# A hybrid attention and linear-attention layer on one core: the first prompt outputs placed later, gate logits in a projection bank, mean squares in PSUM, zero matmuls at the head, later conversions

## The chip, the core and the metric

The kernel runs on one core of a Trainium2 chip. The core has five engines with instruction queues of their own: TensorE (PE in the profile; its weight loads are shown as PEld), VectorE (DVE), ScalarE (ACT), GpSimd (POOL) and SyncE (SP), which issues most of the DMAs. Operands lie in SBUF, matmuls write to PSUM, which here has eight banks of 128 partitions by 512 fp32 numbers. The metric is the time of one execution on the device in microseconds, lower is better; the median of the runs counts.

## What is computed

One step of a one-layer encoder over a prompt of 2048 tokens and a sample of 32, width 1024, all in fp32. Cut to what matters:

```python
def prompt_layer(x, p):
    qa, ka, va, qg, kg, vg, rg, log_a = mixer_inputs(rmsnorm(x, g_mix), w_in, w_alpha, b_alpha, g_q, g_k)
    ...
    attn_o = sink_attend(q_blk, k_band, v_band, sinks, mask)      # 8 query heads, 2 KV heads, window 128, chunks of 64
    gla_o, s_final = gla_chunked(qg, kg, vg, log_a, s0)           # 4 heads, keys 64, values 128, state 64 x 128
    h = x + concat(attn_o, rmsnorm(gla_o, g_gla_out) * silu(rg)) @ w_out
    return h + square(relu(rmsnorm(h, g_ffn) @ w_up)) @ w_down    # 1024 -> 4096 -> 1024
```

`mixer_inputs` is one product with `w_in` (1024 x 2320) whose columns are the attention's q, k and v (512, 128, 128), the linear attention's q, k, v and output gate (256, 256, 512, 512) and 16 columns from which `w_alpha` makes the forget gate: `log_a = log_sigmoid(ca @ w_alpha + b_alpha) / 16`. Queries and keys of the attention get an RMS norm per head. The sample runs the same layer with a cache of 128 keys and a given state.

## The kernel before

Numbers are split in two parts (h and l) and each product takes three matmuls (hh, lh, hl), so that a projection of one tile of 128 tokens over 1024 inputs is 24 matmuls. Tokens go in 16 prompt tiles (0 to 15) and the sample's tile (16).

The program runs through these stages, each recorded with generators that hand control back (`yield`):

- **Attention phase**, to about 368 us. Per tile: `zq` (queries, 24 matmuls of 512 columns), `zkv` (keys, values and the gate's 16 columns, 272 columns of a bank of 512), `zr` (output gate of the linear attention). `self.rsqrt` (L257 to L262) makes the norms of queries and keys by three rounds of small DVE operations on ten numbers a token; its mean squares `ss` lie in an SBUF tile (tag `ssqk`), its scratch in columns 272 to 281 of the zkv bank. `attend(t)` then makes the transposes `qTp` and `kTp`, the scores `S_0` and `S_1` of the two chunks, softmax (`mx`, `negm`, `P`, `es`), the transposes `pT` and the outputs `O`.
- **Linear attention (GLA) phase**, to about 660 us. Eight halves h of two prompt tiles each (h = 0 has the sample's tile in front). Per half: `zq_0`, `zq_1`, `zk_0`, `zk_1`, evacuated by DVE into `kq` (L947), `zv` per tile, evacuated by ACT into `v`; `la`, the gate's logits from `decay(h)`: one bank, evacuated by ACT into `cc`, then log-sigmoid on ACT and a cumulative sum on DVE (L874, L878). Per tile `gla_tile`: decay factors `E` (POOL differences, ACT exponentials, DVE products at L1033 and L1037), the score blocks `A` (104 small matmuls), masked copies into `AT`, output `go` with the state update, and an RMS norm of `go` that writes `g` (L1146) and so empties the banks of `go`; `gTp` transposes `g`.
- **Op phase**, to about 860 us: product with `w_out`, residual, and the second RMS norm, whose square sums are added over partitions by a ones-matmul (`oprb`) and turned by transposes (`rsq_y`).
- **FFN phase**, to 2148 us: up and down products in a Strassen-like scheme of blocks over three groups of tokens; `load_tok` fetches the next group's blocks `T` and ACT and POOL split them into h and l.

What sets the order: `_pe` chains every matmul to the one recorded before it, so TensorE runs in the order of recording. A generator that yields n continues when the matmuls recorded since have a cost of n by the kernel's own counter (`self.clock`, in ns, added to by each matmul recorded). DVE, ACT, POOL and SP take their order from the scheduler. In the first two phases projections take PSUM banks from a pool of three (`ps_m`), everything else from a pool of five (`ps_s`); a tile waits until the last reader of the tile that had the bank is done. Weights and inputs come by DMA through SP's queue; POOL also adds up weight blocks for the FFN (`sd`) and issues its own DMAs.

Of the kernel before, what the change touches and what calls it, by code (L numbers as in the profile page):

```python
# [66 lines left out]
class Builder:  # L67
# [241 lines left out]
    def attention_phase(self):  # L309
# [3 lines left out]
        with ExitStack() as ctx:  # L313
# [56 lines left out]
            V.memset(self.ones, 1.0)  # L370
# [511 lines left out]
    def gla_phase(self):  # L882
        tc, a, V, S, G, Q = self.tc, self.a, self.V, self.S, self.G, self.Q
        nt = self.nt
        with ExitStack() as ctx:
# [375 lines left out]
    def op_phase(self, pool):  # L1261
# [155 lines left out]
        for j, (p, gi) in enumerate(groups):  # L1417
# [37 lines left out]
    def ffn_phase(self):  # L1455
# [4 lines left out]
        with ExitStack() as ctx:  # L1460
# [220 lines left out]
            def load_tok(e, x, engs):  # L1681
# [3 lines left out]
                for i, eng in enumerate(engs):  # L1685
                    ks = slice(i * H // len(engs), (i + 1) * H // len(engs))
                    S.activation(h[:, ks], f32(l[:, ks]), AF.Copy)
                    eng.tensor_tensor(out=l[:, ks], in0=f32(l[:, ks]), in1=f32(h[:, ks]), op=ALU.subtract)
# [424 lines left out]
```

## Time and profile before

| | |
|---|---|
| runs | median 2156.96 us, 2151.72 to 2158.32, 3 runs |
| profiled execution | 2154.14 us, its span 2152.1 us, mean granted TensorE clock 0.995 |
| busy | PE 2121.8 us, DVE 1510.1, ACT 1246.6, POOL 1509.1 |
| DMA | 398.60 MB, mean 185 GB/s |
| end of the attention phase, of GLA, start of the FFN | about 368, 660 and 860 us |

How to read the rows that follow: a row of the timeline has the start and the duration in us, the engine, the line, the operation, "out<-in", sizes, and, in brackets, how long the engine stood idle before it and what it waited for. A row of the table by windows has the busy time of PE, PEld, DVE, ACT and POOL with the count of instructions, then the granted TensorE clock (1.00 is full speed), the DMA share and GB/s. A row of the groups has the busy time, the mean in ns, and the idle time before. Matmuls overlap in the pipeline, so the distance between two starts is what one costs, not its duration.

### The profile page before, as it was taken

The page shows a single profiled execution, that of the slowest core. Times are in us where ns is not written, and L with a number is a line of the kernel's source. Part 1 is how long each engine was busy: PE and PEld are TensorE (multiplying, and loading weights), DVE is VectorE, ACT ScalarE, POOL GpSimd, SP SyncE. Part 2 cuts the span into 40 slices and gives each one's busy share as a digit, 9 for nine tenths or more (in the row PEclk, how much of TensorE's full clock was granted, in tenths as well). Part 3 has the DMA queues.
Part 4 walks back from the last instruction along what each step waited for, and adds up shares of the span by engine and source line. Part 5 has one row for each costly group of instructions (what it writes and reads, how often), then busy time and mean ns, then how long its engine had stood idle before and what let it go on. Part 6 is the DMA issues. An engine that isn't in the chain of part 4 may idle for free.

```text
span 2152.1 us, 40745 instructions
## 1 busy us (share of the span) xinstructions
PE 2121.8 (99%) x14826; PEld 1998.8 (93%) x14826; DVE 1510.1 (70%) x3381; ACT 1246.6 (58%) x2773; POOL 1509.1 (70%) x1423
## 2 busy tenths in 40 slices
PE   8999998999999999999999999999999999999999
PEld 7777786788889999999999999999999999999998
DVE  7777776789897444677777766666666657776665
ACT  6555555665564223766666666656655666666663
POOL 2455656645452667888887887788887768888887
PEclk9999999999999999999999999999999999999999
DMA  7465667353447888755554576444444674444443
GB/s 280 171 206 174 223 225 228 113 170 134 165 149 262 322 339 307 254 176 172 162 161 142 159 257 220 127 136 140 139 140 127 205 260 138 142 151 155 141 127 107
DMA packets 195786, 398.60 MB, mean 185 GB/s; under 512 B 32753, under 2 KB 117922, under 8 KB 188802
## 3 DMA queue, kind: packets, MB, share of 16 engines
q1 hardware_dynamic: 160802, 339.88, 47.0%
q10 hardware_dynamic: 28224, 27.77, 3.8%
q0 software_dynamic: 6560, 28.35, 3.5%
q8 instruction: 117, 1.92, 0.4%
q14 instruction: 83, 0.68, 0.1%
HBM read 290.79 MB, written 105.15 MB: 184 GB/s over the span
## 4 chain that ended last, share of the span: by engine, by line
PE 88%; DVE 4%; ACT 3%; DMA 3%; issue 1%; SPq 0%; ACTq 0%; POOL 0%; DVEq 0%; POOLq 0%
PE dn L171 29%; PE u L171 29%; PE op L171 8%; PE zq L171 4%; PE zr L171 4%; PE zv L171 4%; PE zkv L171 2%; PE zk L171 2%; PE go L171 1%; PE O L171 1%; PE S L171 1%; PE A L171 1%; PE pT L175 1%; DMA wop<-in_w_out 1%; DVE AT L1102 0%
## 5 line engine op out<-in xcount | busy, mean ns | idle before, releaser
L1690 DVE TENSOR_TENSOR P<-P,dn 128x712 f32<-128x712 f32 (+1 forms) x613 | 535.1, 874 | 240.3 <-PE dn L171 224.1
L44 ACT ACTIVATE u<-u 128x356 f32<-128x356 f32 (+1 forms) x384 | 174.0, 453 | 35.9 <-PE u L171 22.9
L44 ACT ACTIVATE r<-u 128x356 f32<-128x356 f32 (+1 forms) x189 | 87.2, 461 | 122.9 <-PE u L171 122.7
L1690 DVE TENSOR_TENSOR u<-u,r 128x356 f32<-128x356 f32 (+1 forms) x144 | 75.8, 526 | 116.4 <-PE u L171 98.8
L1583 POOL TENSOR_TENSOR stage<-stage 128x512 f32<-128x512 f32 x90 | 116.5, 1294 | 20.9 <-DMA stage<-in_w_up 14.2
L795 POOL TENSOR_TENSOR sd<-sd 128x128 f32<-128x128 f32 (+2 forms) x132 | 99.3, 759 | 32.9 <-DMA sd<-in_w_down 29.4
L1026 POOL TENSOR_TENSOR E<-cc 128x256 f32<-128x256 f32 (+1 forms) x117 | 69.6, 630 | 73.4 <-DVE cc L878 24.3
L1102 DVE COPY_PREDICATED AT<-masks,A 64x64 f32<-64x64 int32 (+1 forms) x330 | 82.9, 253 | 17.2 <-ACT AT L44 6.9
L1690 DVE TENSOR_TENSOR uT<-u,uT 128x356 fp32r<-128x356 f32 (+1 forms) x183 | 90.1, 511 | 2.9 <-ACT uT L44 2.7
L44 ACT ACTIVATE uT<-u 128x356 fp32r<-128x356 f32 (+1 forms) x187 | 81.7, 458 | 3.3 <-DVE u L1690 2.8
L1690 DVE TENSOR_TENSOR uB<-u,uB 128x356 fp32r<-128x356 f32 (+1 forms) x141 | 72.4, 513 | 14.1 <-ACT u L44 13.9
L44 ACT ACTIVATE op<-y 128x356 f32<-128x356 f32 (+1 forms) x42 | 19.6, 468 | 96.5 <-DVE y L1430 96.4
L1430 DVE TENSOR_TENSOR y<-op,y 128x356 f32<-128x356 f32 (+1 forms) x48 | 25.2, 532 | 68.2 <-PE op L171 63.6
L44 ACT ACTIVATE P<-S,negm 128x192 f32<-128x192 f32 (+2 forms) x128 | 51.5, 417 | 36.3 <-DVE negm L656 30.3
L44 ACT ACTIVATE E<-E 128x1024 f32<-128x1024 f32 (+2 forms) x68 | 67.2, 1012 | 1.1
L44 ACT ACTIVATE uB<-u 128x356 fp32r<-128x356 f32 (+1 forms) x141 | 64.5, 458 | 2.9
L1037 DVE TENSOR_TENSOR E<-E,kq 128x256 f32<-128x256 f32 (+1 forms) x117 | 57.3, 542 | 0.6 <-ACT E L44 0.5
L44 ACT ACTIVATE v<-go 128x256 f32<-128x256 f32 (+1 forms) x34 | 12.8, 380 | 66.2 <-DVE Sp L1134 32.7
L620 POOL COPY VB<-v 64x64 f32<-64x64 f32 x64 | 15.0, 234 | 49.2 <-ACT v L44 47.1
L44 ACT ACTIVATE pS<-pT 128x256 f32<-128x256 f32 (+1 forms) x62 | 27.5, 488 | 32.0 <-PE pT L175 31.9
L655 DVE TENSOR_REDUCE mx<-S 128x2 f32<-128x384 f32 (+2 forms) x64 | 32.8, 536 | 18.5 <-PE S L171 18.1
L1690 DVE TENSOR_TENSOR u<-u,f 128x356 f32<-128x356 f32 (+1 forms) x86 | 44.7, 519 | 1.4 <-ACT u L44 1.4
(1577 smaller groups left out, 8158.4 us busy)
## 6 DMA issues: line engine op xcount, KB each, us to landing
stage<-in_w_up SPq DMA_DIRECT2D x90, 512.0 KB, 4.3
stage<-sd SPq DMA_DIRECT2D x86, 512.0 KB, 4.5
stage<-in_w_down SPq DMA_DIRECT2D x43, 512.0 KB, 3.3
stage<-su SPq DMA_DIRECT2D x30, 512.0 KB, 4.1
stage<-in_w_down SPq DMA_DIRECT2D x47, 256.0 KB, 3.4
sd<-sd POOLq DMA_DIRECT2D x11, 1024.0 KB, 5.3
x1a<-in_x_prompt SPq DMA_DIRECT2D x16, 512.0 KB, 6.2
wod<-wop SPq DMA_DIRECT2D x16, 512.0 KB, 3.1
```

The lines of the kernel that those rows point to most:

```text
L44: ins = f(*args, **kw)
L171: self._pe(self.T.matmul(out, lhsT, rhs, start=start, stop=stop, **kw), ns)
L175: self._pe(self.T.transpose(out=out, in_=in_, identity=self.ident[:r, :r]), 109)
L620: G.tensor_copy(vb[hp, ch, cs], v[ch * 64 : ch * 64 + 64, cs])
L655: V.reduce_max(mx[:, ch, us], sp, axis=AX.X)
L795: self.after(self.G.tensor_tensor(out=o, in0=x, in1=y, op=op), self.last_pe)
L1026: G.tensor_tensor(out=e4, in0=c4, in1=ref, op=ALU.subtract)
L1037: V.tensor_tensor(out=e4, in0=e4, in1=halves_of(kq, L, m), op=ALU.mult)
L1102: V.copy_predicated(dst, mk.unsqueeze(1).broadcast_to([L // nh, 2, w // m, m]), src[r].rearrange("s p (n m) -> s p n m", m=m),)
L1430: self.after(V.tensor_tensor(out=y[:, f], in0=ps, in1=y[:, f], op=ALU.add), self.last_state if j == 0 else None)
L1583: tt = lambda o, x, y, op: G.tensor_tensor(out=o, in0=x, in1=y, op=op)
L1690: add = lambda out, x, y, op=ALU.add: V.tensor_tensor(out=out, in0=x, in1=y, op=op)
```

## The change

Eight edits.

1. *Head.* A tile of zeros is cleared by DVE, and three fp32 matmuls of 128 x 384 on it stand ahead of the first projection; their result is not used. The transposed input of the first two tiles comes in four pieces of two k-slices each instead of two of four.
2. *Mean squares.* `ss` of the query and key norms lies in columns 288 to 297 of the zkv bank, in PSUM.
3. *Attention's last tile.* `attend(15)` yields 11000 instead of 8500.
4. *GLA's first prompt tile.* The step that makes `go_0` yields 13000 instead of 10000.
5. *Gate logits.* For halves of 256 tokens `la` takes a bank of the pool of three (`ps_m`).
6. *Op phase.* In the second of its groups (j = 1) the three steps of the norm of the group before stand behind output blocks 2, 3 and 5.
7. *Conversions.* `load_tok` issues the DMA as before, but the splits of the next group's blocks are recorded four units later.
8. *End.* The two halves of the last unit have banks of their own.

```diff
@@ attention phase, head
+            warm = self.mid.tile([P, 576], F32, tag="cc", name="warm")[:, :512]
+            V.memset(warm, 0.0)
+            idle = self.ps_s("idle")
+            for _ in range(3):
+                self.mm(idle[:, :384], warm[:, :P], warm[:, :384], True, True)
...
-            half = [slice(0, 4), slice(4, KB)]
-            fetch_x = lambda t, i: Q.dma_start(xT[t][:, half[i]], a["xT_prompt"][t, :, half[i]])
+            two = [slice(k, k + 2) for k in range(0, KB, 2)]
+            fetch_x = lambda t, i: Q.dma_start(xT[t][:, two[i]], a["xT_prompt"][t, :, two[i]])
...
+            for i in range(KB // 2):
+                fetch_x(0, i)
+                fetch_q(2 * i)
+                fetch_x(1, i)
+                fetch_q(2 * i + 1)
@@ norms of queries and keys
-                ss = self.small.tile([P, 10], F32, tag="ssqk", name=f"ssqk_{t}")[:r]
+                ss = bank[:r, 288:298]
@@ attend
-                yield 8500 if t else 12500
+                yield {0: 12500, nt - 1: 11000}.get(t, 8500)
@@ decay
-            x = self.ps_s(f"la_{h}")
+            x = self.ps_m(f"la_{h}")
@@ gla_tile
-                yield 10000 if t != nt - 1 else 5000
+                yield 5000 if t == nt - 1 else 13000 if first else 10000
@@ op phase
-                if f in ((1, 2, 4) if gi else (1, 2, 5)) and pending is not None:
+                if f in ((2, 3, 5) if j == 1 else (1, 2, 4) if gi else (1, 2, 5)) and pending is not None:
@@ FFN phase
+            def load_tok(e, x, engs, delay=0):
                 h, l = e.T[x]
                 Q.dma_start(f32(l), self.Td[e.p][x])
...
+                if delay:
+                    fresh.append([delay, convert])
+                else:
+                    convert()
...
-                        load_tok(envs[n + 1], t, (G, G))
+                        load_tok(envs[n + 1], t, (G, G), 4)
...
+                        if end:
+                            ps = [x.tile([P, 512], F32, tag="b", name=f"dn{g}_{q}_{j}").unsqueeze(1) for x in ps1[:2]]
...
                 merge_some(g % NF, i, x)
+                convert_due()
```

Where the moved steps stand now. First TensorE's rows at the end of the attention phase; `S_1` is tile 14's, `qTp` and `kTp` are tile 15's. Before:

```order
L171 MATMUL S_1_0_4375<-kW_4233,qT_4227 128x192
L171 MATMUL S_1_1_4376<-kW_4233,qT_4227 128x192
L175 MATMUL qTp_4397<-packed,qk_4128 128x128 x4
L175 MATMUL kTp_4402<-packed,kn_4259 128x128
L175 MATMUL kTp_4402<-packed,CA_385 96x128
L171 MATMUL zr_4370<-wr0h,nT_14h 128x512
L171 MATMUL zr_4370<-wr0l,nT_14h 128x512
```

and of the change, where the first three zr rows shown are the last of twelve behind S_1:

```order
L171 MATMUL zr_4363<-wr1h,nT_14h 128x512
L171 MATMUL zr_4363<-wr1l,nT_14h 128x512
L171 MATMUL zr_4363<-wr1h,nT_14l 128x512
L175 MATMUL qTp_4405<-packed,qk_4122 128x128 x4
L175 MATMUL kTp_4410<-packed,kn_4252 128x128
L175 MATMUL kTp_4410<-packed,CA_395 96x128
L171 MATMUL zr_4363<-wr1h,nT_14h 128x512
```

Twelve zr matmuls have come between the scores of tile 14 and the transposes of tile 15. Behind them S_0 of tile 15 stands after pT_1 of tile 14, S_1 after zq_1, and la after that, ahead of all 24 zk_0.

Next TensorE's rows at the first prompt tile of GLA (`go_0` is tile 0's output, `A_1` tile 1's score blocks). Before:

```order
L171 MATMUL A_1_5245<-E_0_4955 64x32
L171 MATMUL go_0_5266<-v_4872,AT_4697 128x128
L171 MATMUL go_0_5267<-v_4872,AT_4697 128x128
L171 MATMUL go_0_5266<-v_4872,AT_4697 128x128
L171 MATMUL go_0_5267<-v_4872,AT_4697 128x128
L171 MATMUL go_0_5267<-v_4872,kdT_5029 64x128 x4
L171 MATMUL A_1_5244<-E_0_4955 64x32
```

and of the change:

```order
L171 MATMUL A_1_5238<-E_1_4959 64x32
L171 MATMUL zv_5346<-wvg0h,nTb_1h 128x512
L171 MATMUL zv_5346<-wvg0l,nTb_1h 128x512
L171 MATMUL zv_5346<-wvg0h,nTb_1l 128x512
L171 MATMUL zv_5346<-wvg0h,nTb_1h 128x512
L171 MATMUL zv_5346<-wvg0l,nTb_1h 128x512
L171 MATMUL zv_5346<-wvg0h,nTb_1l 128x512
L171 MATMUL go_0_5356<-v_4865,AT_4690 128x128
```

The last 32 rows of A_1 and six of zv now stand ahead of go_0.

Last TensorE's rows at `la` of h = 5, with the queues each row waits for in brackets. Before:

```order
L171 MATMUL A_8_7137<-E_1_6968 64x32
L171 MATMUL la_7218<-caf_7083,wal 128x256 [waits DMAHW6_49,DMAHW7_49,DVE_49,Activation_49]
L171 MATMUL la_7218<-caf_7083,wal 128x256
L175 MATMUL gTp_7231<-packed,g_6167 128x128 [waits DVE_49,Activation_49]
L175 MATMUL gTp_7231<-packed,g_6167 128x128 x3
L171 MATMUL dk_7241<-ones,qkp_7044 64x2 [waits Activation_49]
```

and of the change:

```order
L171 MATMUL A_8_7127<-E_1_6957 64x32
L171 MATMUL la_7207<-caf_7074,wal 128x256 [waits DMAHW7_49,DMAHW0_49,Activation_49]
L171 MATMUL la_7207<-caf_7074,wal 128x256
L175 MATMUL gTp_7221<-packed,g_6168 128x128 [waits DVE_49]
L175 MATMUL gTp_7221<-packed,g_6168 128x128 x3
L171 MATMUL dk_7231<-ones,qkp_7032 64x2 [waits DVE_49,PE_49]
```

The wait for DVE has gone from la to gTp. On the same tiles POOL's `sd` rows have moved: ahead of this place a group of seven stands as two, the store of the block, its load, and three.

More of the change, by code (lines that the diff above doesn't have):

```diff
@@ L1679, in prepare, with convert, convert_due @@
                 next(makers[x, g])
-            def load_tok(e, x, engs):
+            fresh = []
+            def load_tok(e, x, engs, delay=0):
                 h, l = e.T[x]
                 Q.dma_start(f32(l), self.Td[e.p][x])
[L1685 to L1688, printed above, removed]
+                def convert():
+                    for i, eng in enumerate(engs):
+                        ks = slice(i * H // len(engs), (i + 1) * H // len(engs))
+                        self.after(S.activation(h[:, ks], f32(l[:, ks]), AF.Copy), self.last_pe if delay else None)
+                        eng.tensor_tensor(out=l[:, ks], in0=f32(l[:, ks]), in1=f32(h[:, ks]), op=ALU.subtract)
+                if delay:
+                    fresh.append([delay, convert])
+                else:
+                    convert()
+            def convert_due():
+                for x in fresh:
+                    x[0] -= 1
+                while fresh and fresh[0][0] <= 0:
+                    fresh.pop(0)[1]()
             add = lambda out, x, y, op=ALU.add: V.tensor_tensor(out=out, in0=x, in1=y, op=op)
@@ L1805, in down @@
                     units = []
+                    end = g == total - 1 and i == 4
                     for (q, *terms), j in UNITS[i]:
-                        ps = ps2[j // 2].tile([P, 2, 512], F32, tag="two", name=f"dn{g}_{q}_{j}")
-                        units.append((q, terms, j, ps))
-                    end = g == total - 1 and i == 4
+                        if end:
+                            ps = [x.tile([P, 512], F32, tag="b", name=f"dn{g}_{q}_{j}").unsqueeze(1) for x in ps1[:2]]
+                        else:
+                            x = ps2[j // 2].tile([P, 2, 512], F32, tag="two", name=f"dn{g}_{q}_{j}")
+                            ps = [x[:, y : y + 1] for y in range(2)]
+                            both = x
+                        units.append((q, terms, j, ps, None if end else both))
                     def part(unit, f, k):
-                        q, terms, j, ps = unit
+                        q, terms, j, ps, _ = unit
                         fs = slice(f * P, (f + 1) * P)
@@ L1816, in part @@
                         uh, ul = e.B11 if x == "B11" else e.U[x]
-                        self.mm3(ps[:, f - j, : e.N], wh[:, fs], wl[:, fs], uh, ul, not k, bool(k))
+                        self.mm3(ps[f - j][:, 0, : e.N], wh[:, fs], wl[:, fs], uh, ul, not k, bool(k))
                     def fold(unit, f, m):
-                        q, _, j, ps = unit
+                        q, _, j, ps, both = unit
                         y = e.acc[q][:, f : f + m]
-                        add(y, y, ps[:, f - j : f - j + m, : e.N])
+                        add(y, y, (ps[f - j] if m == 1 else both)[:, :, : e.N])
                         if g == total - 1:
```

10 lines of the change are left out of this document (removed).

## Prediction

> **What bounds the kernel now.** I read the page first: the busy shares, then the chain that ended last.
>
> ```profile
> PE 2121.8 (99%) x14826; PEld 1998.8 (93%) x14826; DVE 1510.1 (70%) x3381; ACT 1246.6 (58%) x2773; POOL 1509.1 (70%) x1423
> PE 88%; DVE 4%; ACT 3%; DMA 3%; issue 1%; SPq 0%; ACTq 0%; POOL 0%; DVEq 0%; POOLq 0%
> ```
>
> TensorE is busy for 2121.8 of 2152.1 us, and the change takes no work from it (it adds three matmuls). So it can win only TensorE's 30.3 idle us, and time in which TensorE works at a lower clock. Next I went through the timeline of PE for rows with an idle time in brackets. Outside the head these are the longest, and one of those between:
>
> ```profile
> 340.39 0.33 PE L175 MATMUL kTp<-packed,kn 128*128 128x128 f32 x1 [2.44 <-ACT P L44]
> 412.47 1.04 PE L171 MATMUL go<-v,AT 128*128 128x128 f32 x5 [2.47 <-DVE g L1146]
> 546.10 0.77 PE L171 MATMUL la<-caf,wal 96*128 96x256 f32 x2 [2.46 <-issue]
> 705.54 0.67 PE L171 MATMUL oprb<-packed,rsq_y_y 82*128 82x82 f32 x4 [1.20 <-DVE rsq_y_y L262]
> 1723.50 0.80 PE L171 MATMUL dn<-uB,wf_d15A 128*128 128x356 f32 x2 [2.13 <-ACT u L44]
> 2146.83 0.72 PE L171 MATMUL dn<-f,wf_d15A 128*128 128x328 f32 x3 [0.66 <-DVE P L1690]
> ```
>
> Then the table by windows, laid just behind the first five (column before the last two: granted clock):
>
> ```profile
> 340.83:344.83 4.00, 4.00 (x12) 3.10 (x12) 2.99 (x11) 4.00 (x18) 3.31 (x4) 0.57 0.69 250
> 412.94:419.50 6.56, 6.56 (x84) 5.36 (x83) 4.15 (x18) 3.48 (x11) 4.01 (x8) 0.50 0.37 117
> 546.00:552.90 6.90, 6.80 (x36) 6.48 (x37) 6.40 (x24) 5.46 (x9) 0.58 (x2) 0.51 0.32 100
> 705.50:709.50 4.00, 3.96 (x28) 3.96 (x29) 3.19 (x8) 0.45 (x1) 4.00 (x4) 1.00 0.60 210
> 1723.40:1727.40 4.00, 3.90 (x15) 3.93 (x15) 2.30 (x5) 3.22 (x7) 3.13 (x2) 0.57 1.03 410
> ```
>
> The reader is to see that a gap costs more than itself: after each gap of 2.13 us or more the clock is halved for a while, after the one of 1.20 it is not. Window times (1 - clock) gives the extra loss: 4.00 x 0.43 = 1.7, 6.56 x 0.50 = 3.3, 6.90 x 0.49 = 3.4, and 1.7 at 1723. So the gaps at 340, 412 and 546 cost 4.1, 5.8 and 5.9 us, and these are the terms to look at.
>
> **The change part by part.** All sums are against the profiled run: 2154.1 us (span 2152.1 and 2.0 around it).
>
> *Tile 15's transposes, 12 zr matmuls later.* TensorE stood before kTp for P of tile 14. In the new order 12 zr matmuls come first.
>
> ```profile
> 333.33 0.92 PE L171 MATMUL S<-kW,qT 64*128 64x192 f32 x8
> 334.18 0.50 PE L171 MATMUL zr<-wr1h,nT_14h 128*128 128x512 f32 x1
> 336.44 0.92 PE L171 MATMUL S<-kW,qT 64*128 64x192 f32 x8
> ```
>
> Between the two S groups lie nine zr matmuls, 334.18 to 336.44: 0.25 us each. Twelve are 3.0 us, more than the 2.44 of the wait, so the wait and its slow clock go: **-4.1**. The mean squares in PSUM help here, because the DVE was late with the maximum on which P rests:
>
> ```profile
> L260 DVE TENSOR_TENSOR zkv<-ssqk,rsq_y_qk 128x10 f32<-128x10 f32 x48 | 17.0, 356 | 1.0
> L260 DVE TENSOR_TENSOR go<-go,rsq_y_g 128x4 f32<-128x4 f32 x48 | 8.0, 168 | 1.1
> 328.50 2.17 DVE L260 TENSOR_TENSOR zkv<-ssqk,rsq_y_qk 128x10 f32<-128x10 f32 x1
> 328.25 2.38 POOL L285 TENSOR_TENSOR wqgl<-stage,wqgh 128x1024 fp32r<-128x1024 f32 x1
> ```
>
> The op that reads ssqk and y from SBUF takes 356 ns, the same op with one side in PSUM 168, and its long cases (2.17 us) lie beside a POOL op of like length. 48 x 0.188 = 9.0 us of DVE time go. DVE is not the bound in attention, so I add nothing for it; it pays only where TensorE waits, which the 4.1 holds already (bounds: 0, and the attention waits that I leave standing below).
>
> The price of the move is a later tail of attention. There the trace shows
>
> ```profile
> 364.38 0.65 PE L171 MATMUL O<-pS,v 128*64 128x256 f32 x4 [0.99 <-ACT pS L44]
> 366.78 0.65 PE L171 MATMUL O<-pS,v 128*64 128x256 f32 x4 [0.47 <-ACT pS L44]
> 368.93 0.40 PE L171 MATMUL zk<-nTb_0h,wkgh 128*128 128x288 f32 x1 [0.87 <-DVE kq L947]
> 360.63 0.91 ACT L44 ACTIVATE cc<-la,packed 128x288 f32<-128x288 f32 x2
> 361.63 0.69 ACT L44 ACTIVATE la<-cc 128x576 f32<-128x576 f32 x1
> 363.75 0.85 ACT L44 ACTIVATE pS<-pT 128x512 f32<-128x512 f32 x2
> 364.73 1.41 DVE L878 TENSOR_TENSOR_SCAN cc<-d,la 128x288 f32<-128x288 f32 x2
> ```
>
> three waits, 2.33 us. In the new order the last scores S_1 of tile 15 stand behind zq_1, with la and 24 zk_0 before the first pT. From the end of S_1 on: mx, negm, es on DVE 1.3 us; on ACT cc (0.91), four P (1.7), es, and two la steps (0.69 each) are queued before pS, which so ends 5.6 us after S_1; TensorE gets to its O after la, zk_0 and pT in 4.2: a wait of 1.4. The next O waits some 0.95 (pS, 0.85, behind pT), and zk_1 waits for scan and kq for 1.1. Together 3.45: **+1.1** (bounds: 0, and +3, with a slow clock if one of them passes 2.13). The step's other work moves with it: kW on ACT and POOL, the copies of v on POOL, and the mix stores on the ACT queue, which the op phase alone reads.
>
> *First prompt output of GLA later.* go_0 moves behind the 32 last A_1 matmuls and six zv; it needs g of the sample's tile out of the bank.
>
> ```profile
> 411.57 1.10 DVE L1146 SCALAR_TENSOR_TENSOR g<-go,rsq_y_g,g 32x128 f32<-32x128 f32 x4
> 541.83 1.82 PE L171 MATMUL A<-E 64*64 64x64 f32 x104
> ```
>
> The 32 are 64 records: 64 x 1.82/104 = 1.1; six zv of 0.25 are 1.5; 2.6 us of cover, just the 2.47 of the wait: -2.5 - 3.3 = **-5.8** (bounds: 0, if the wait only moves along, and that). Behind go_0 on TensorE stand the rest of zv; the state update and the norm of tile 0 on DVE follow 2.6 us later, beside projections that don't need them, and so do the copies on ACT and the stores of tile 0, which only the op phase reads, past 620 us.
>
> *la in a projection bank.* At 546.10 la waited for a bank of go_7, which DVE's g frees at 546.27; the row's "issue" hides that. Now la takes a bank that ACT has emptied, but gTp behind it takes over the same wait on DVE, as the order's waits show. So only la's own 0.57 (546.10 to the gTp at 546.67) is covered, and 1.89 us could stay, between 1.20 and 2.13. But DVE was late there because of
>
> ```profile
> 541.50 2.67 DVE L1037 TENSOR_TENSOR E<-E,kq 128x256 f32<-128x256 f32 x3
> 540.61 5.81 POOL L795 TENSOR_TENSOR sd<-sd 128x256 f32<-128x256 f32 x7 [4.14 <-DMA sd<-in_w_down]
> 546.18 1.26 DVE L1037 TENSOR_TENSOR E<-E,kq 128x256 f32<-128x256 f32 x3
> ```
>
> the same three ops take 2.67 beside POOL's sd and 1.26 alone. In the new order two of these seven stand before the DMA that the others wait for, so the rest starts about 1.5 us later and shorter. I take the gap as short enough to leave the clock alone: -0.57 - 3.4 = **-4.0** (bounds: 0, and -5.9).
>
> *Second output step of the op phase (j = 1).* The ones-matmul and the transposes move 24 matmuls later. The window at 705.50 has 28 records in 3.96 us, 0.14 each: 24 are 3.4, more than 1.20: **-1.2** (bounds: 0, if DVE's sums come as much later, and that).
>
> *Last unit in two banks.* The last half of the unit no longer waits for the fold of the first: **-0.7** (bounds: 0 and that).
>
> *Head.* Three zero matmuls and smaller x pieces.
>
> ```profile
> 5.30 0.80 PE L171 MATMUL zq<-wq0h,nT_0h 128*128 128x512 f32 x1 [5.30 <-ACT wq0h L44]
> 9.63 0.63 PE L171 MATMUL zq<-wq0h,nT_0l 128*128 128x512 f32 x1
> 10.06 0.45 PE L171 MATMUL zq<-wq0h,nT_0h 128*128 128x512 f32 x1
> 0.81 0.06 DVE L370 MEMSET ones<- 128x1 f32 x1 [0.81 <-PEq L2102]
> 37.51 0.50 PE L171 MATMUL zq<-wq0h,nT_2l 128*128 128x512 f32 x1 [0.98 <-POOL nT_2l L350]
> ```
>
> Until 10.06 a zq takes 0.43 us; the zr above, also of 512 columns, took 0.25. Eleven at the slow pace cost 2.0 us, the most to be won. A zero matmul isn't in this trace. From S (four matmuls, eight records, in 0.85 us: 0.21 for 192 columns at full clock) 384 columns at half clock take 0.85, or twice that for weights twice as wide. DVE begins at 0.81 and must clear the tile first; from about 1.4 on, three of them end between 4.0 and 6.5, so they cost up to 1.2 at 5.30. What is won is partly lost to the wait for nT_2l at 37.51, which hangs on DMA, ACT and POOL, and SP issues four more DMAs ahead of the weights. I take **-0.7** (bounds -2.0, +1.2).
>
> *Later conversions.* At 1723.50 the converted T1h still stands ahead of the squared u on ACT, so I give **0** (bounds -3.8, 0).
>
> [...]
>
> Sum: -4.1 + 1.1 - 5.8 - 4.0 - 1.2 - 0.7 - 0.7 = -15.4, so 2138.7 for a run like the profiled one. The median before is 2.8 above that run; I add half of it: **2140.1**.
>
> **The rivals.**
> 1. *gTp keeps the long wait at 546* and the slow clock with it. For: the wait itself isn't removed, 1.89 is nearer to 2.13 than to 1.20. Against: POOL's lighter load. +3.4: 2143.5.
> 2. *GLA gives it back.* DVE is nearly full there:
>
> ```profile
> 522.00:546.00 24.00, 21.27 (x227) 17.31 (x226) 22.73 (x68) 13.01 (x24) 17.02 (x25) 1.00 0.52 190
> ```
>
> 22.73 of 24 us. If TensorE comes 9 us earlier and DVE does not, two new gaps like that of 412 (2.47 + 3.3 = 5.8 each) appear: +11.6, 2151.7. Against: DVE mostly waits for TensorE in the windows before.
> 3. *Slower: seven tiles on three projection banks.* zk_0 takes la's bank, so it must wait for ACT's cc.
>
> ```profile
> 511.01 0.84 ACT L44 ACTIVATE cc<-la,packed 128x256 f32<-128x256 f32 x2
> 513.84 0.28 PE L171 MATMUL zk<-nTb_4h,wkgh 128*128 128x256 f32 x1
> ```
>
> The margin is 513.84 - 511.85 = 2.0 us here. If ACT comes later than that against TensorE by another 2.47 in five of the seven halves, each costs 5.8: +29.0, 2169.1. From three on the gain is gone.
> 4. *The gap at 1723 goes too* (u is ready earlier): -3.8, 2136.3.
> 5. *The slow clock doesn't hang on the gaps*: 1.7 + 3.3 + 3.4 stay, 2148.5. [...]
>
> **How the numbers follow.** Forecast 0.42; rivals 0.20, 0.20, 0.10, 0.06, 0.02. A measurement of this kernel tells about 0.3% (6.5 us) from no change, so faster means below 2150.5 and slower above 2163.4: the forecast and rivals 1, 4 and 5 are faster (0.70), rival 2 is the same (0.20), rival 3 slower (0.10). The range leaves out rival 3. Its low end is rival 4 with the tail's 1.1 and the head's other 1.3 won and 1.9 us for the scatter of runs, 2132; its high end is rival 2 and 2.3 us for the scatter, 2154.
>
> **What would show it.** kTp of tile 15 without a wait and clock 1.00 after it; go_0 of the first tile with a wait under 1 us; gTp of the first tile of h = 5 with a wait under 2 us and no half clock; oprb without 1.20; the last dn without 0.66; 1723 as before. The forecast is wrong if new gaps over 2 us stand at zk_0, zk_1 or O between 345 and 660, or if half clock remains with the gaps gone.

## Result, and the profile after

| | before | after |
|---|---|---|
| median of 6 runs | 2157.02 us | 2168.37 us (2163.02 to 2172.5) |
| ratio after/before, 95% interval | | 1.006 [1.0047, 1.0072] |
| profiled execution, its span | 2154.14, 2152.1 | 2163.02, 2160.9 |
| start of `la` of h = 1, of h = 7, end | 392.40, 618.63, 2152.1 | 393.40, 626.94, 2160.9 |
| from h = 1 to h = 7 (most of GLA) | 226.23 | 233.54 |

The change made the kernel slower by 0.6%, where the prediction said faster by 0.8% (2140.1 us, range 2132 to 2154). The last two lines of the table say where: `la` of h = 1 stands 1.0 us later, GLA from there takes 7.3 us more, and all that follows 0.5 us more (up to FFN's first `u` 2.6 us more, from there 2.1 less). The profiled execution is the shortest of the six after, so it shows 8.8 of the 11.4 us between the medians. It is also the one with the highest mean granted clock: 0.996, where the six lie between 0.990 and 0.996. So the trace shows the added waits better than what the clock adds in the other runs.

The page's shares and chain after:

```profile
PE 2124.1 (98%) x14832; PEld 1997.2 (92%) x14832; DVE 1508.8 (70%) x3382; ACT 1246.5 (58%) x2773; POOL 1508.0 (70%) x1423
PE 78%; DVE 11%; DMA 5%; ACT 4%; issue 2%; POOL 1%; SPq 0%; ACTq 0%; DVEq 0%; POOLq 0%
```

TensorE's own share of the chain has fallen from 88 to 78%, DVE's has grown from 4 to 11%. TensorE's busy time hardly changed (2121.8 before, with 4.2 us of zero matmuls in the 2124.1 now): what grew is waiting, from 30.3 to 36.8 us, and DVE is what most of it waits for. The timeline of PE after, at the places that the prediction looked at and at the two that it did not:

```profile
343.27 0.66 PE L175 MATMUL pT<-packed,P 128*128 128x128 f32 x4 [0.87 <-POOL P L674]
357.54 0.40 PE L171 MATMUL la<-caf,wal 96*128 96x288 f32 x1 [0.94 <-ACT P L44]
365.38 0.65 PE L171 MATMUL O<-pS,v 128*64 128x256 f32 x4 [2.79 <-ACT pS L44]
369.93 0.40 PE L171 MATMUL zk<-nTb_0h,wkgh 128*128 128x288 f32 x1 [0.86 <-DVE kq L947]
413.49 0.71 PE L171 MATMUL go<-v,AT 128*128 128x128 f32 x4 [0.15 <-DVE g L1146]
431.13 0.41 PE L175 MATMUL dk<-packed,E 128*128 128x128 f32 x2 [3.68 <-DVE AT L1049]
552.13 0.51 PE L171 MATMUL la<-caf,wal 96*128 96x256 f32 x2
623.47 0.41 PE L175 MATMUL dk<-packed,E 128*128 128x128 f32 x2 [2.08 <-DVE go L261]
720.08 1.12 PE L171 MATMUL oprb<-packed,rsq_y_y 82*128 82x82 f32 x8 [1.81 <-DVE rsq_y_y L262]
1734.83 1.38 PE L171 MATMUL dn<-uB,wf_d15A 128*128 128x356 f32 x7 [0.82 <-ACT u L44]
```

and the table by windows behind them (column before the last two: granted clock):

```profile
343.00:347.00 4.00, 3.73 (x26) 3.45 (x27) 3.90 (x5) 2.42 (x4) 4.00 (x5) 1.00 0.25 98
413.50:420.00 6.50, 6.50 (x36) 5.36 (x37) 5.94 (x24) 4.15 (x5) 5.37 (x8) 1.00 0.71 258
431.00:447.00 16.00, 14.96 (x171) 12.81 (x172) 10.80 (x36) 9.73 (x20) 5.54 (x10) 0.57 0.27 79
624.00:628.00 4.00, 4.00 (x114) 3.77 (x112) 3.52 (x12) 1.54 (x7) 0.00 (x0) 0.60 0.12 46
1734.00:1738.00 4.00, 3.18 (x21) 3.21 (x21) 2.18 (x4) 2.78 (x7) 2.81 (x2) 1.00 1.03 417
```

The gaps of 340 and 546 are gone, the one of 412 has shrunk to 0.15 us, and the half clock behind them is gone too (1.00 over 552 to 560 as well). In their place stands, besides the 2.79 us at `O` that the last section comes back to, one row that was no gap before: `dk` at 431.13 waits 3.68 us, and 16 us at clock 0.57 follow, 16 x 0.43 = 6.9 us. Together 10.6 us, against the 5.8 us that `go_0` saved. A second gap at a `dk` stands at 623.47 (2.08 + 4 x 0.40 = 3.7). 10.6 + 3.7 - 5.8 = 8.5 is near GLA's 7.3.

The `dk` rows at 431.13 are the transposes of the decay factors of tile 2 (`self.tr` behind `yield 4000` at L1054). They go into the bank whose diagonal DVE reads with the copy at L1049, so they wait for that copy. The timeline of DVE after, some rows of 413 to 432:

```profile
414.29 1.51 DVE L1102 COPY_PREDICATED AT<-masks,A 64x64 f32<-64x64 int32 x6
...
416.29 3.77 DVE L1102 COPY_PREDICATED AT<-masks,A 64x64 f32<-64x64 int32 x13
...
422.30 0.61 DVE L1134 SCALAR_TENSOR_TENSOR Sp<-Sp,ec,go 128x128 f32<-128x128 f32 x2
...
425.90 0.68 DVE L1141 TENSOR_REDUCE go<-v 128x4 f32<-128x512 f32 x1
...
429.23 1.13 DVE L1146 SCALAR_TENSOR_TENSOR g<-go,rsq_y_g,g 128x128 f32<-128x128 f32 x4
430.27 0.71 DVE L1049 COPY_PREDICATED AT<-packed,dk 128x512 f32<-128x512 int32 x1
```

No row of DVE in this stretch has an idle time (17.98 us busy of the 19 from 413 to 432). Ahead of the copy for `dk` it does all masked copies of tile 1 (L1102), the state update of tile 0 (L1134) and tile 0's whole norm (L1141 to L1146). And the same places before, DVE first, then PE:

```profile
414.82 0.61 DVE L1134 SCALAR_TENSOR_TENSOR Sp<-Sp,ec,go 128x128 f32<-128x128 f32 x2 [1.48 <-PE go L171]
415.93 0.69 DVE L1141 TENSOR_REDUCE go<-v 128x4 f32<-128x512 f32 x1 [0.51 <-ACT v L44]
...
429.07 1.12 DVE L1146 SCALAR_TENSOR_TENSOR g<-go,rsq_y_g,g 128x128 f32<-128x128 f32 x4
...
431.78 0.72 DVE L1049 COPY_PREDICATED AT<-packed,dk 128x512 f32<-128x512 int32 x1
```

```profile
431.87 0.43 PE L175 MATMUL gTp<-packed,g 32*128 32x32 f32 x4
432.23 0.51 PE L171 MATMUL la<-caf,wal 96*128 96x256 f32 x2
432.66 0.49 PE L171 MATMUL go<-Sp,Qc 64*128 64x128 f32 x4
...
435.38 0.66 PE L175 MATMUL gTp<-packed,g 128*128 128x128 f32 x4
435.87 0.38 PE L175 MATMUL dk<-packed,E 128*128 128x128 f32 x2
```

`go_0` itself ends at about 415 us in both traces. But its state update on DVE now starts 7.5 us later (422.30 for 414.82) and its norm 10.0 us later (425.90 for 415.93), because the copies of tile 1, whose `A_1` is now complete ahead of `go_0`, stand in front of them. Before, the copy for `dk` came 1.5 us later than after, and nobody waited: `gTp`, `la`, all of `go_1` and the next `gTp` stood ahead of `dk`, 4.0 us of TensorE work that waited for nothing. After, the PE timeline reads the other way round:

```profile
431.47 0.89 PE L171 MATMUL A<-E 64*64 64x64 f32 x40
432.29 0.43 PE L175 MATMUL gTp<-packed,g 32*128 32x32 f32 x4
432.65 0.80 PE L171 MATMUL la<-caf,wal 96*128 96x256 f32 x2
```

TensorE's recorded order here, with the number of matmuls (`dk1` is the ones-matmul behind which the copy at L1049 stands, `dkE` the transposes that wait for the copy):

```
before: A_1 20, go_0 8, A_1 32, zv 42,       dk1 4, zv 6,  zq_0 18, gTp 4, la 2, go_1 12, gTp 4, dkE 2, A_2 20
after:  A_1 52, zv 6, go_0 8, zv 30,         dk1 4, zv 12, zq_0 18, dkE 2, A_2 20, gTp 4, la 2, go_1 12, A_2 32
```

`gTp`, `la` and `go_1` stand where they stood against the projections. But `dk1` comes six zv earlier than before, and the 4000 that `dkE` counts from it now run out just ahead of `gTp` instead of just behind `go_1`. So a step that the change doesn't name has passed 22 matmuls that covered it. That this is the cause is a theory from two traces; the experiments test it.

### The profile page after: what moved, and what is told of

It reads as the page before. It is cut to its first block, busy times and chain, and to the rows that moved or that the text cites. A ratio compares the mean times of both kernels' runs of the same rounds, so it can differ in the third digit from the quotient of the medians.

```text
span 2160.9 us, 40744 instructions
## 1 busy us (share of the span) xinstructions
PE 2124.1 (98%) x14832; PEld 1997.2 (92%) x14832; DVE 1508.8 (70%) x3382; ACT 1246.5 (58%) x2773; POOL 1508.0 (70%) x1423
## 4 chain that ended last, share of the span: by engine, by line
PE 78%; DVE 11%; DMA 5%; ACT 4%; issue 2%; POOL 1%; SPq 0%; ACTq 0%; DVEq 0%; POOLq 0%
PE dn L171 28%; PE u L171 28%; PE op L171 7%; PE zr L171 3%; DVE AT L1102 3%; PE zq L171 3%; PE zkv L171 2%; DVE E L1037 2%; PE O L171 1%; DMA stage<-in_w_in 1%; PE S L171 1%; PE zv L171 1%; PE pT L175 1%; PE go L171 1%; DVE g L1146 1%
## 5 line engine op out<-in xcount | busy, mean ns | idle before, releaser
L1102 DVE COPY_PREDICATED AT<-masks,A 64x64 f32<-64x64 int32 (+1 forms) x330 | 82.9, 253 | 19.7 <-ACT AT L44 9.5
```

The source lines that it names most:

```text
L1102: V.copy_predicated(dst, mk.unsqueeze(1).broadcast_to([L // nh, 2, w // m, m]), src[r].rearrange("s p (n m) -> s p n m", m=m),)
```

## Experiments

All ratios are against runs of the kernel before on the same chip, with a 95% interval; the median of these runs lay between 2153.6 and 2155.2 us. Where two ratios from different chips are compared, both errors count. "GLA" is the time from `la` of h = 1 to `la` of h = 7 in the one profiled execution (226.23 before, 233.54 after).

| kernel | what it is | us | ratio | GLA |
|---|---|---|---|---|
| e1_go | change without edit 4 | 2155.86 | 1.0011 [1.0001, 1.0020] | 225.93 |
| e2_la | change without 5 | 2166.31 | 1.0057 [1.0044, 1.0070] | |
| e3_go_la | change without 4 and 5 | 2156.84 | 1.0013 [1.0003, 1.0023] | |
| e4_attend | change without 3 | 2166.67 | 1.0061 [1.0047, 1.0075] | |
| e5_b4 | before with 4 alone | 2165.66 | 1.0062 [1.0044, 1.0080] | 235.21 |
| e6_g11 | change, `go_0` at 11000 | 2156.34 | 1.0008 [0.9995, 1.0022] | 221.37 |
| e7_gdk | change, `dk` of tile 2 later too | 2160.22 | 1.0031 [1.0014, 1.0048] | 228.42 |
| e9_dke | change without 4, `dk` of tile 2 early | 2167.80 | 1.0057 [1.0040, 1.0074] | 232.06 |
| e8_a346 | change without 3, 4, 6 | 2158.33 | 1.0020 [1.0011, 1.0030] | |
| e10_b78 | before with 7 and 8 | 2153.51 | 0.9995 [0.9981, 1.0009] | 225.60 |
| e12_b45g78 | before with 5, 7, 8 and `go_0` at 11000 | 2153.57 | 0.9997 [0.9983, 1.0010] | 226.61 |
| e11_b1 | before with 1 alone | 2161.51 | 1.0030 [1.0021, 1.0039] | 226.08 |
| e13_warm | before with the zero matmuls alone | 2155.43 | 1.0004 [0.9994, 1.0014] | 225.81 |
| e14_pieces | before with the x pieces alone | 2161.41 | 1.0032 [1.0020, 1.0045] | 226.68 |
| e15_no14 | change without 1 and 4 | 2151.99 | 0.9982 [0.9972, 0.9991] | 225.67 |
| e16_no1g | change without 1, `go_0` at 11000 | 2148.89 | 0.9976 [0.9961, 0.9990] | 221.35 |

### Which edit holds the loss: e1_go, e2_la, e3_go_la, e4_attend

Edits 4, 5, both, and 3 are taken back, one kernel each. Against the change:

```diff
e1_go, e3_go_la:
-                yield 5000 if t == nt - 1 else 13000 if first else 10000
+                yield 10000 if t != nt - 1 else 5000
e2_la, e3_go_la:
-            x = self.ps_m(f"la_{h}")
+            x = self.ps_s(f"la_{h}")
e4_attend:
-                yield {0: 12500, nt - 1: 11000}.get(t, 8500)
+                yield 8500 if t else 12500
```

> The change without its edit 4 (go_0 back to 10000). Theory T1: the loss sits in edit 4, because the decay transposes (dk) of tile 2 now stand ahead of go_1 and meet DVE before it has emptied their bank (the 3.68 us gap at 431 and the half clock behind it), and GLA does not recover. Then this kernel has no gap over 2 us at the dk of tile 2, has the wait of about 2.5 us at go_0 again, and is 6 to 10 us faster than the change. T2 (the loss sits in edit 5, la in a projection bank): within 3 us of the change, with the gaps past 470 us still there. T3 (edit 3, attention's tail): within 3 us of the change.

> The change without its edit 5 (la back in the pool of five). T1: within 3 us of the change, the gap at 431 stays. T2: 6 to 10 us faster, the gaps between 470 and 680 us (1.0 at 486, 1.2 at 524, 2.1 at 623, 1.2 at 661) go.

> The change without edits 4 and 5. T1: like the run without edit 4 alone, to 2 us. T2: like the run without edit 5 alone. If both share the loss, it is faster than either, and near the kernel before or up to 4 us below it, as the gains past 700 us stay.

> The change without its edit 3 (attend of tile 15 back to 8500). T1 and T2: the wait before kTp at 340 comes back and those at 357 and 365 shrink, so within 2 us of the change. T3: 4 us or more faster, all of it ahead of 370 us.

Without edit 4 the ratio falls from 1.0060 to 1.0011 and GLA from 233.54 to 225.93; without 5 or without 3 nothing moves. So edit 4 holds the greater part of the loss, and the theories that put it on la's bank or on the tail of attention fell. Two more readings come from here. The timelines of PE of e3_go_la and of e1_go at h = 5, where edit 5 was to pay:

```profile
548.15 0.49 PE L171 MATMUL la<-caf,wal 96*128 96x256 f32 x2 [2.10 <-ACT AT L44]
```

```profile
550.34 0.66 PE L175 MATMUL gTp<-packed,g 128*128 128x128 f32 x4 [1.71 <-DVE g L1146]
```

Without edit 5 `la` waits 2.10 us; with it `gTp` behind it waits 1.71, and both show the same clock in the next 8 us, 0.79. This is the prediction's first rival, in the kernel without edit 4. In the changed kernel the gap at `la` is gone for another reason: TensorE comes there 6 us late (552.13), and in e2_la, which has `la`'s old bank, `la` doesn't wait either (555.52).

The timeline of PE of e4_attend, where edit 3 is undone:

```profile
341.01 0.33 PE L175 MATMUL kTp<-packed,kn 128*128 128x128 f32 x1 [1.42 <-ACT P L44]
365.54 1.05 PE L171 MATMUL O<-pS,v 128*64 128x256 f32 x4 [2.24 <-ACT pS L44]
```

The wait at `kTp` is back, though with 1.42 in place of 2.44 us and clock 1.00 behind it (341 to 345), and the tail's wait is 2.24 in place of 2.79. What edit 3 takes at 340 it gives back in other waits, and the ratio doesn't move.

### What edit 4 does: e5_b4, e6_g11, e7_gdk, e9_dke

```diff
e5_b4, against before (edit 4 alone):
-                yield 10000 if t != nt - 1 else 5000
+                yield 5000 if t == nt - 1 else 13000 if first else 10000
e6_g11, against the change (go_0 behind all A_1, ahead of zv; dk of tile 2 stays behind go_1):
-                yield 5000 if t == nt - 1 else 13000 if first else 10000
+                yield 5000 if t == nt - 1 else 11000 if first else 10000
e7_gdk, against the change (L1054):
-                yield 4000
+                yield 4000 + 3000 * (t == 2)
e9_dke, against e1_go (L1054):
-                yield 4000
+                yield 4000 - 1000 * (t == 2)
```

> The kernel before with edit 4 alone (go_0 at 13000). T1: the loss comes with edit 4 whatever else is there: the decay transposes (dk) of tile 2 stand ahead of go_1 and wait for DVE 3 us or more, with half clock behind, and the time is 7 to 13 us above the kernel before. If edit 4 loses only together with the other edits, it is within 3 us of the kernel before, or below it.

> The change with go_0 at 11000 instead of 13000: go_0 then stands behind all of A_1 but ahead of zv, and the dk of tile 2 stays behind go_1, as in the kernel before. T1: no wait over 1 us at that dk; go_0 waits 2.45 - 1.1 = 1.3 us, too short for the half clock, so 4 to 6 us faster than the run without edit 4 (near 2151), and 14 us faster than the change. If it is the later go_0 itself that loses (its later DVE work), then this kernel lies between the change and the run without edit 4.

> The change with go_0 at 13000, but the decay transposes of tile 2 yielded 3000 later, so that they stand behind go_1 and its gTp again. T1 (the place of dk loses): the 3.7 us gap and its half clock go, 8 us or more faster than the change. If the later go_0 loses through DVE's later work: no faster than 3 us below the change, with a gap of like size at another row of GLA.

> The change without edit 4, but with the decay transposes of tile 2 yielded 3000 instead of 4000, so that they and a first part of A_2 stand ahead of la and go_1, as edit 4 puts them, while go_0 stays where the kernel before has it. T1: their place alone loses: a wait of 2 us or more at this dk, half clock behind it, and 3 us or more above the run without edit 4 (2155.9 there). T4 (the later go_0 loses, through the later work of DVE): within 2 us of that run.

e5_b4 has the whole loss by itself. Its timeline of PE and its window:

```profile
436.96 0.66 PE L175 MATMUL dk<-packed,E 128*128 128x128 f32 x2 [4.49 <-DVE AT L1049]
```

```profile
436.90:452.00 15.10, 14.14 (x160) 11.78 (x161) 9.07 (x31) 8.66 (x20) 3.66 (x7) 0.50 0.27 66
```

4.49 + 15.1 x 0.50 = 12.0 us at one place, less the 5.8 that `go_0` no longer waits. This profile is of the slowest of the six runs (2175.23 us, the median is 2165.66), so it shows the loss larger than it usually is.

e7_gdk keeps the late `go_0` and puts `dk` back behind `go_1` and `gTp`: no wait at that `dk`, and 1.0060 becomes 1.0031. That is some 6 of the 8 us that the expectation asked for, and not all of edit 4's loss. What is left stands at `go_1`, which now meets DVE's late norm and has clock 0.66 over 430 to 440:

```profile
429.93 0.49 PE L171 MATMUL go<-Sp,Qc 64*128 64x128 f32 x2 [1.51 <-DVE g L1146]
```

e9_dke is the other half: `go_0` where it was before, only `dk` early (here behind `gTp`, ahead of `la` and `go_1`). It loses as much as the change, 1.0057 against e1_go's 1.0011. But not as the expectation had it: no wait of 2 us stands at the `dk`, and no half clock behind it (1.00 over 432 to 470). The timeline of PE:

```profile
437.46 0.41 PE L175 MATMUL dk<-packed,E 128*128 128x128 f32 x2 [0.76 <-DVE AT L1049]
443.78 0.32 PE L171 MATMUL A<-E 64*64 64x32 f32 x8 [1.00 <-issue]
446.03 0.40 PE L171 MATMUL dk<-ones,qkp 128*64 128x2 f32 x8 [1.35 <-ACT gT L44]
...
588.95 0.41 PE L175 MATMUL dk<-packed,E 128*128 128x128 f32 x2 [1.71 <-DVE AT L1049]
```

The wait is spread over many places. All of GLA in one window, first e1_go, then e9_dke (the columns are the busy times of PE, PEld, DVE, ACT and POOL):

```profile
410.00:670.00 260.00, 252.53 (x3089) 217.09 (x3088) 232.91 (x782) 153.37 (x294) 122.42 (x176) 0.97 0.46 160
```

```profile
410.00:670.00 260.00, 247.73 (x2952) 212.90 (x2951) 232.39 (x764) 150.47 (x284) 119.59 (x180) 0.97 0.43 149
```

DVE is busy for the same 232 of 260 us in both, though it gets 18 fewer of its operations done, and TensorE is busy for 4.8 us less. How far each half of GLA takes shows where the time goes (us from `la` to `la`, one trace each):

| kernel | h = 1 to 2 | h = 2 to 3 | h = 3 to 7 |
|---|---|---|---|
| before | 39.83 | 39.27 | 147.13 |
| the change | 39.25 | 45.43 | 148.86 |
| e1_go | 41.04 | 39.26 | 145.63 |
| e7_gdk | 34.34 | 44.28 | 149.80 |
| e9_dke | 41.68 | 40.93 | 149.45 |
| e6_g11 | 37.14 | 39.99 | 144.24 |

In the change most of the loss lies in the half with the long wait. e7_gdk comes to h = 2 in 5.5 us less than before and gives 5.0 of it back in the next half, about what the 1.51 us at `go_1` and 10 x 0.34 = 3.4 us by the clock behind it make: TensorE comes sooner, DVE does not. e9_dke loses 1.7 us in the half of its `dk`, against e1_go, and 3.8 in the halves behind; a reading that fits is that TensorE runs closer on DVE's heels there, but how an early `dk` costs time so late was not shown.

So two experiments bear on the place of `dk`. To take it away wins back 0.29 of the 0.49% (e7_gdk), and to bring it without a later `go_0` costs 0.46% (e9_dke against e1_go). That the place of `dk` costs is shown; that it costs through the one long wait is shown for the change, not for e9_dke. The rest of edit 4's loss is about 0.2%; where it shows best is `go_1`, behind DVE's late norm. The yield of 11000 (e6_g11) moves `go_0` less far, and `dk` stays behind `go_1` and `gTp`: GLA falls to 221.37, with a `go_0` wait of 1.53 us instead of 2.47. But the gain of 4 to 6 us over e1_go that was expected did not come: 1.0008 against 1.0011, and the slow clock behind `go_0` stayed (0.72 over 6 us, last section).

### The other edits, and the head: e8_a346, e10_b78, e12_b45g78, e11_b1, e13_warm, e14_pieces

Edits 3, 4 and 6 undone (e8); to the kernel before are added 7 and 8 (e10); 5, 7, 8 and e6_g11's yield (e12); 1 (e11); and the two parts of 1 by themselves (e13, e14):

```diff
e8_a346, against the change, besides the lines of e1_go and e4_attend:
-                if f in ((2, 3, 5) if j == 1 else (1, 2, 4) if gi else (1, 2, 5)) and pending is not None:
+                if f in ((1, 2, 4) if gi else (1, 2, 5)) and pending is not None:
e13_warm, against before:
+            warm = self.mid.tile([P, 576], F32, tag="cc", name="warm")[:, :512]
+            V.memset(warm, 0.0)
+            idle = self.ps_s("idle")
+            for _ in range(3):
+                self.mm(idle[:, :384], warm[:, :P], warm[:, :384], True, True)
e14_pieces, against before:
-            half = [slice(0, 4), slice(4, KB)]
+            two = [slice(k, k + 2) for k in range(0, KB, 2)]
...
+            for i in range(KB // 2):
+                fetch_x(0, i)
+                fetch_q(2 * i)
+                fetch_x(1, i)
+                fetch_q(2 * i + 1)
```

> The change without edits 3, 4 and 6 (head, mean squares in PSUM, la's bank, later conversions and the end remain). The run without edit 4 lost what edits 3 and 6 should have won: 6.9 us of waits at the end of attention where the kernel before had 4.8, and 1.8 us before oprb where it had 1.2. If these two edits are worth nothing or cost a little, this kernel is 0 to 4 us faster than the run without edit 4; if edit 3 is worth its 3 us, it is slower than that run by 2 to 4 us.

> The kernel before with edits 7 and 8 alone. By the traces of the change the wait at 1723 falls from 2.13 to 0.4 to 1.6 us, mostly without half clock, and the 0.66 of the end goes: 2 to 4 us below the kernel before. If the half clock at 1723 was chance, less than 2 us.

> A candidate: the kernel before with edits 5, 7 and 8 and go_0 at 11000. The wait at go_0 falls from 2.47 to 1.4, the one at 546 to under 2, 1723 and the end as in the run with edits 7 and 8: if the half clock of these gaps goes too, 8 to 12 us below the kernel before; if it stays at half of them, 4 to 6.

> The kernel before with edit 1 alone (zero matmuls and smaller x pieces). The prediction has it 0.7 us below the kernel before; the traces of the change show the clock's gain given back to waits for weights and x up to 38 us: within 2 us of the kernel before, on either side.

> The kernel before with the three zero matmuls alone. Theory H1 (the zero matmuls cost: they hold TensorE past 5.3 us, and what comes later doesn't give it back): 2 to 6 us above the kernel before. H2 (the smaller x pieces cost: more DMAs ahead of the weights): within 2 us of the kernel before.

> The kernel before with the x pieces of two k-slices alone. H1: within 2 us of the kernel before. H2: 2 to 6 us above it, with the load of mx0l issued 9.6 us behind that of y in the op phase (6.0 before) and a wait of over 3 us at oprb.

Edits 7 and 8 can't be told from nothing (0.9995), where 2 to 4 us were expected, and e12_b45g78, expected 4 to 12 us faster than before, isn't either (0.9997): its `go_0` waits 1.54 us, and a `dk` at 543.61 waits 2.70. Edits 3 and 6 together, e8_a346 against e1_go, make 1.0020 to 1.0011, with intervals that overlap. The surprise is edit 1: 0.30% slower by itself, and all of it from the x pieces (1.0032), none from the zero matmuls (1.0004). Most of it is not lost in the head: from `la` of h = 7 to FFN's first `u` the kernel before takes 237.7 us, e11_b1 243.0, e14_pieces 243.3, and e13_warm 237.9. The place lies some 700 us into the run; e11_b1's timelines of PE, of ACT and of SP:

```profile
711.16 2.00 PE L171 MATMUL oprb<-packed,rsq_y_y 82*128 82x82 f32 x8 [3.86 <-DVE rsq_y_y L262]
```

```profile
704.46 2.86 ACT L44 ACTIVATE mx0h<-mx0l 128x712 fp32r<-128x712 f32 x4 [2.88 <-DMA mx0l<-mix]
```

```profile
687.24 0.37 SPq L60 DMA_DIRECT2D y<-in_x_group  x1
696.88 0.34 SPq L60 DMA_DIRECT2D mx0l<-mix  x1
```

and SP before:

```profile
684.27 2.03 SPq L60 DMA_DIRECT2D y<-in_x_group  x1
690.28 0.34 SPq L60 DMA_DIRECT2D mx0l<-mix  x1
```

Read from the bottom: SP issues the load of `mx0l` 9.6 us behind the load of `y` instead of 6.0, ACT's split of it waits for the data, the copies for the residual queue behind the split on ACT, DVE's norm steps stand behind an addition that waits for them, and `oprb` waits 3.86 us (1.20 before). The window there has clock 0.72, so 2.7 us more wait and 12 x 0.28 = 3.4 by the clock, near the 6.5 us of the ratio:

```profile
708.00:720.00 12.00, 8.84 (x43) 8.84 (x44) 7.26 (x21) 2.02 (x5) 10.27 (x8) 0.72 1.01 377
```

e14_pieces shows the same (3.89). In the changed kernel edit 6 covers part of it and leaves 1.81 (3.89 in e8_a346, which has the pieces and not edit 6). The traces show one step more. The load of `mx0l` reads what the store `mix<-gT` writes, and SP waits for that store: 3.9 us before, 9.1 in e11_b1 and e14_pieces. ACT issues the store 0.56 us ahead of the load of `y` in both, but `mx0l` follows the store after 6.6 us before and after 10.2 us in e11_b1. Before, SP is held for 2.0 us at the load of `y` by an ACT copy; in e11_b1 that load goes out at once (0.37). So it is in every trace here: in twelve the load of `y` takes 0.37 or 0.38 us to issue, and `mx0l` follows 9.5 to 9.8 us behind it; in six it takes 1.1 to 2.3, and `mx0l` follows after 5.7 to 6.6. That the load of `y` delays the store is the likely reading, but no run moved that load alone. Why the pieces let it go out sooner stays open; e5_b4, which has no pieces, shows the same (0.37 and 9.55 us), so the pieces are one way into it, not the only one.

### The rest of the change by itself: e15_no14, e16_no1g

The change without the head, with `go_0` as before (e15) or at 11000 (e16): the head's lines of e13_warm and e14_pieces and the line of e1_go, or of e6_g11, are taken back or set.

> The change without edits 1 and 4. If edit 1 ate the gain of the others: 4 to 8 us faster than the run without edit 4 alone, so 2 to 6 us below the kernel before. If the others have no gain: within 2 us of the run without edit 4.

> The change without edit 1 and with go_0 at 11000. As the run without edits 1 and 4, less up to 4 us if the shorter wait at go_0 leaves the clock alone; the same if the half clock follows a wait of 1.5 us as often as one of 2.5.

Edits 2, 3, 5, 6, 7 and 8 together gain 0.18% (e15_no14), about 4 us. e16_no1g is faster than before by 0.24% (2148.89 against 2155.24 us, its interval 0.10 to 0.39%), and faster than the change by about 0.8%. Between e15 and e16 the intervals overlap, so what 11000 adds is seen in GLA (221.35 against 225.67) more surely than in the ratio; in e12_b45g78, which also has the 11000 but not edits 2 and 3, GLA did not fall (226.61).

Measured one by one, the parts add up within the noise: -0.18% (e15_no14) and +0.30% for edit 1 alone (e11_b1) make +0.12%, and e1_go, which has both, measured +0.11%. With the +0.62% of edit 4 alone (e5_b4) that makes +0.74%, where the change measured +0.60% (0.47 to 0.72).

## Why the prediction was wrong

The forecast was -15.4 us, the medians say +11.4, a miss of 27. By terms:

| step | forecast | what the runs show |
|---|---|---|
| `go_0` later (edit 4) | -5.8 | +0.49%, 10.5 us (change less e1_go; alone 0.62%) |
| head (edit 1) | -0.7 | +0.30%, 6.5 us (e11_b1) |
| mean squares (edit 2) | 0 | the op of L260 takes 173 ns on average in place of 356 (its median was 178 before: the long cases are gone), 8.1 us in all in place of 17.0; not run alone |
| 340 and the tail (edit 3) | -4.1 + 1.1 | -0.01 +- 0.19% (the change less e4_attend) |
| la's bank (edit 5) | -4.0 | -0.02 and +0.03% (e1_go less e3_go_la, the change less e2_la) |
| `oprb` (edit 6) | -1.2 | wait 1.20 to 1.81, as the pieces make it 3.9; without them no wait is left (e15_no14, e16_no1g) |
| end (edit 8) | -0.7 | its gap of 0.66 us is gone: no row of PE from 2140 us on has a wait after |
| conversions (edit 7) | 0 | gap at 1723 from 2.13 to 0.82, the clock behind it from 0.57 to 1.00; 7 and 8 together -0.05 +- 0.14% |

**Edit 4.** The step that failed is "Behind go_0 on TensorE stand the rest of zv; the state update and the norm of tile 0 on DVE follow 2.6 us later, beside projections that don't need them". The first half of the term was right: `go_0`'s wait fell from 2.47 to 0.15 us and the clock behind it is 1.00. But on DVE the state update follows 7.5 us later and the norm 10.0 us later, the copy for `dk` stands behind both, and on TensorE `dk` moved ahead of the 22 matmuls that had covered it. The prediction followed the moved step and what stands behind it; it did not list which steps of other tiles, counted by their own yields, change places. Its second rival ("GLA gives it back", two gaps of 5.8) named the right place, a DVE nearly full that doesn't come earlier with TensorE, as e7_gdk shows; it had no step that changes places. One gap with its half clock cost 10.6 us, nearly twice a gap of 412.

**Edit 1.** "I take -0.7 (bounds -2.0, +1.2)" looked only at the first 40 us. There the result lies inside the bounds, but on the other side: the `zq` that waits for `nT_2l` starts at 38.41 in place of 37.51. The zero matmuls ran and TensorE came to its full pace earlier (a `zq` every 0.23 us from 6.23 on, before from 10.06 on); waits for the weights and for `nT_2` (0.87, 0.71 and 0.69 us) took it back. Its row after:

```profile
1.46 4.21 PE L171 MATMUL idle<-warm 128*128 128x384 f32 x6 [1.46 <-DVE ones L780]
```

They end at 5.67, inside the 4.0 to 6.5 that was forecast. That the split of the x loads makes a load of the op phase late, and costs 6.5 us, was in no bound.

**Edit 3.** The step is "Together 3.45". Measured are 2.79, 0.47 and 0.86, and 0.94 and 0.40 at `la` and 0.87 at `pT` besides, 6.33 in all, where 2.33 stood before: +4.0 in place of +1.1. The mechanism was as described: on ACT, `cc`, four `P` and two `la` steps stand ahead of `pS`. But the sum left out what else stands there: the four `P` of `S_0`, two weight splits (1.07 and 0.65 us) and a copy (0.60). TensorE reached its `O` 6.0 us after S_1 (4.2 forecast), at 362.59, and `pS` let it go after 8.8 (5.6 forecast), at 365.38. The size was wrong, and it eats the -4.1.

**Edit 5.** "I take the gap as short enough to leave the clock alone" failed: in e1_go `gTp` kept 1.71 us (1.89 had been worked out) and the clock was 0.79 over 8 us. This is rival 1, given 0.20. (One reading there is off by little: the 546.27 is the end of the last of four `g` operations, and `la`, which started at 546.10, can only have waited for one before it.)

**The clock.** The premise that a gap of 1.20 leaves the clock alone and one of 2.13 halves it was read from five rows, and five rows were too few; see the last section. Rival 3 (`zk_0` behind ACT's `cc`) did not come: no row of PE in GLA after with a wait over 0.5 us is a `zk_0`. Rival 4 came true in the trace for the most part (0.82 us of the gap stay), yet its 3.8 us can't be seen in the ratio of e10_b78.

## What to carry to other kernels

When a step is moved in a program whose order comes from counters, list everything that changes place against it, not only what stands behind it: here most of the loss of edit 4 came from a step that the change doesn't name, which slipped ahead of its cover. Ask of each covered wait which rows cover it, and whether they still stand ahead of it. And try the parts of a change apart: of these eight edits two cost 0.8% and the others gained 0.2%.

## What the hardware showed that was not expected

In these traces the length of a gap alone does not say whether the clock is halved behind it. The plainest pair is `go_0` at 11000: it waits 1.53 us in e6_g11 and in e16_no1g, on the same row. The windows behind it, first e6_g11, then e16_no1g:

```profile
415.50:421.50 6.00, 5.97 (x27) 4.88 (x28) 5.44 (x22) 0.38 (x1) 5.10 (x8) 0.72 0.71 243
```

```profile
415.50:421.50 6.00, 6.00 (x34) 4.92 (x35) 5.47 (x23) 0.41 (x2) 4.64 (x7) 1.00 0.62 215
```

Likewise the 2.79 us at `O` near 365 left the clock at 1.00 in the change and in e7_gdk, and in e1_go 0.72 over 6 us followed it; behind 1.82 us in e1_go (`oprb` at 712.44) and 1.81 us in the change (`oprb` at 720.08) it stayed at 1.00. How long the slow stretch lasts varies too: put as time at clock 0.50, the windows shown amount to between 3 us (4 x 0.40 / 0.50 at 624 in the change) and 15 us (15.1 at 0.50 in e5_b4).

No fixed length of idling fits these rows: 1.51 us (`go_1` in e7_gdk) and 1.53 us (`go_0` in e6_g11) have a clock of 0.66 and 0.72 behind them, 1.53 us (`go_0` in e16_no1g) and 2.79 us (`O` in the change) one of 1.00. What else decides it was not shown. A price per gap is therefore an average: one trace of this kernel, whose six runs lie between 2163.02 and 2172.5 us, shows one of its outcomes.

The zero matmuls bought nothing (1.0004 in e13_warm). There they end as the first `zq` starts, at 5.53 and without a wait (5.30 before), and at 7.37 and 7.60 two stand 0.23 us apart, the pace that is reached from 10.06 on before. But the seventh `zq` waits 1.12 us for `wq0h`, and the clock is halved behind it: 0.79 over 8 to 16 us, with a `zq` every 0.43 us from 9.84 to 13.24.

```profile
9.11 0.51 PE L171 MATMUL zq<-wq0h,nT_0h 128*128 128x512 f32 x1 [1.12 <-ACT wq0h L44]
```

In the change and in e11_b1, where the x pieces are smaller, the granted clock stays at 1.00 there. In the head that column has to be read with care: before, it shows 1.00 from 0 to 16 us, though a `zq` takes 0.43 us up to 10.06 and 0.23 from there on.
